# Row maxima on one core: loads of equal size from two queues in place of loads of shrinking size from one

## The chip, the cores and the metric

The kernel runs on one core of a Trainium2 chip. The metric is the device time of one execution in microseconds, taken as the median over runs. A profiled execution also has a span: the time from its first to its last recorded instruction, which is a little shorter than its device time.

## What is computed

The input has 32 x 512 x 1024 float32 values (67.11 MB). The output is the maximum over the last dimension, 32 x 512 float32 values (65.5 KB):

```
batch, seq, dim = 32, 512, 1024
x = np.random.randn(batch, seq, dim).astype(np.float32)
out = np.max(x, axis=-1).astype(np.float32)
```

There are 16,384 rows of 1024 values, and each row is read once. In what follows "a row" is a row per partition: 128 rows of the input, one on each of the 128 partitions, 4 KB each, 0.524 MB in all.

## The kernel before, in words

The 16,384 rows are dealt out so that partition p holds rows 128p to 128p+127; on each partition there are I = 128 rows to reduce, and a load of g rows reads 4g KB of contiguous memory for each partition.

The kernel is one loop over the list ROWS (line 12), which has 27 entries that begin at 10 and 13 and shrink to 1; they sum to 127. For each entry it does two things. Line 47 issues one load of g rows from SP's queue, into the next g rows of a ring of 46 rows in on-chip memory (RING, line 13; when fewer than g rows are left at the ring's end, it starts again at the ring's beginning). Line 48 reduces these g rows on VectorE (DVE) to g columns of the tile `res`. The last row is loaded in two halves of 512 values (line 58), each half is reduced by itself (line 59), and one instruction takes the larger of the two (line 60).

Two stores leave from the Activation engine's queue (ACT): line 53 stores the first 112 columns of `res` once the first 112 rows have been reduced, and line 64 stores the last 16 at the end.

Nobody writes the order of the engines by hand. A framework tracks which instruction reads and writes which part of which tile and puts in the waits. Three kinds matter here. A reduction waits for the landing of its own load. A load waits, in the queue that issues it, until the reductions that read the part of the ring it will overwrite have ended. And the framework counts landings on eight semaphores that it hands out in turn to all loads and stores, so a load also waits for the landing of the transfer eight before it. Instructions of one queue are issued in order: one that waits holds up those behind it.

Of the kernel before, what the change touches and what calls it, by code (L numbers as in the profile page):

```python
# [1 line left out]

# [4 lines left out]


F32 = mybir.dt.float32


ROWS = [10, 13, 12, 10, 9, 8, 7, 7, 6, 5, 5, 4, 4, 3, 3, 3, 3, 2, 2, 2, 2, 2, 1, 1, 1, 1, 1]
RING = 46


@with_exitstack
def kernel(
    ctx: ExitStack,
    tc: tile.TileContext,
    x: bass.AP,  # L20
    out: bass.AP,
):
    nc = tc.nc
    P = 128
    X = mybir.AxisListType.X

    xf = x.flatten_outer_dims()
    N, D = xf.shape
    H = D // 2
    I = N // P  # L30

    xr = xf.rearrange("(p i) d -> p i d", p=P)
    of = out.flatten_outer_dims()
    out_r = bass.AP(tensor=of.tensor, offset=of.offset, ap=[[I, P], [1, I]])

    once = ctx.enter_context(tc.tile_pool(name="once", bufs=1))
    ring = once.tile([P, RING, D], F32)
    res = once.tile([P, I], F32)
    part = once.tile([P, 2], F32)

    b = at = 0
    stored = 0
    for g in ROWS:
        if at + g > RING:
            at = 0
        xc = ring[:, at:at + g, :]
        nc.sync.dma_start(out=xc, in_=xr[:, b:b + g, :])
        nc.vector.reduce_max(out=res[:, b:b + g], in_=xc, axis=X)  # L48
        at += g
        b += g  # L50
        if not stored and b >= I - 16:
            stored = b
            nc.scalar.dma_start(out=out_r[:, :b], in_=res[:, :b])

    assert b == I - 1 and at + 1 <= RING
    for h in range(2):
        xh = ring[:, at, h * H:(h + 1) * H]
        nc.sync.dma_start(out=xh, in_=xr[:, b, h * H:(h + 1) * H])
        nc.vector.reduce_max(out=part[:, h:h + 1], in_=xh, axis=X)  # L59
    nc.vector.tensor_tensor(  # L60
        out=res[:, b:b + 1], in0=part[:, 0:1], in1=part[:, 1:2],
        op=mybir.AluOpType.max,
    )
    nc.scalar.dma_start(out=out_r[:, stored:], in_=res[:, stored:])


# [1 line left out]
_INS = ['x']  # L68
_OUTS = [((32, 512), 'float32')]


# [23 lines left out]
```

## Time and profile before

| what | us |
|---|---|
| median of 3 runs | 166.39 |
| lowest and highest of the runs | 165.94, 166.50 |
| device time of the profiled execution | 166.5 |
| span of the profiled execution | 164.7 |
| DVE busy within the span | 139.5 |
| DVE idle ahead of the reductions, waiting for loads | 22.7, in 6 waits |

In the profile, DVE is VectorE, SPq and ACTq are the queues from which SP and the Activation engine issue transfers, and `ring<-in_x_dram` is a load from the input into the tile `ring`. A row of the timeline has the start, the duration, the engine, the line of the code, the operation, its output and input with their shapes, and a count where several like instructions were merged into one row; brackets at its end tell how long the engine had been idle and what ended that. In the rows on DMA queues there are the number of packets, the MB and the share of the time of the 16 DMA engines that these packets took. q1 is SP's queue, q10 is ACT's. One load of g rows is 144 packets: 128, one for each partition, and 16 small ones that report completion. A row of the groups by shape has the total and the mean duration (ns) of its instructions and the idle time ahead of them.

### The profile page before, as it was taken

To read this page: it belongs to the slowest core of one execution; us is meant where nothing else is said; L and a number is where in the kernel's file an instruction comes from. 1 tells how busy PE (TensorE), PEld (TensorE's weight loads), DVE (VectorE), ACT (ScalarE), POOL (GpSimd) and SP (SyncE) were. 2 spreads that over 40 slices of the span, in tenths; PEclk is the share of its full clock that TensorE was granted. 3 is DMA by queue.
4 is the path that set the end of the run, shared out by engine and by line. 5 is a ranking of instruction groups with operands and counts; after the bars stand their busy time and mean duration, and the time that the engine had idled before them with its cause. 6 is when DMAs were issued, how large, how long until landed. Compare 5 with 4: busy or idle time off the path is not lost.

```text
span 164.7 us, 118 instructions
## 1 busy us (share of the span) xinstructions
DVE 139.5 (85%) x30; POOL 0.2 (0%) x4
## 2 busy tenths in 40 slices
DVE  0001994399989999999999989999999999999994
POOL 0000000000000000000000000000000000000000
DMA  6998999999989999999999999999999999999960
GB/s 199 438 467 376 453 465 453 436 406 394 469 388 467 444 430 430 408 438 425 439 432 425 426 431 419 428 438 409 438 430 421 427 421 421 420 418 421 408 260 2
DMA packets 4464, 67.18 MB, mean 408 GB/s; under 512 B 752, under 2 KB 752, under 8 KB 1648
## 3 DMA queue, kind: packets, MB, share of 16 engines
q1 hardware_dynamic: 4176, 67.11, 95.8%
q10 hardware_dynamic: 288, 0.07, 0.2%
HBM read 67.11 MB, written 0.07 MB: 408 GB/s over the span
## 4 chain that ended last, share of the span: by engine, by line
DMA 70%; DVE 28%; issue 0%
DMA ring<-in_x_dram 70%; DVE res L48 27%; DVE part L59 1%; DVE res L60 0%
## 5 line engine op out<-in xcount | busy, mean ns | idle before, releaser
L48 DVE TENSOR_REDUCE res<-ring 128x2 f32<-128x2048 f32 (+11 forms) x27 | 138.1, 5165 | 22.9 <-DMA ring<-in_x_dram 22.7
L59 DVE TENSOR_REDUCE part<-ring 128x1 f32<-128x512 f32 x2 | 1.3, 676 | 0.0
L60 DVE TENSOR_TENSOR res<-part 128x1 f32<-128x1 f32 x1 | 0.2, 159 | 0.0
L79 POOL MEMSET const-bfloat16-1.0<- 128x1 bf16 x1 | 0.1, 101 | 0.0
L79 POOL MEMSET const-uint8-127<- 128x1 uint8 x1 | 0.1, 101 | 0.0
L79 POOL MEMSET const-float32-0.0<- 128x1 f32 x1 | 0.1, 98 | 0.2 <-issue 0.2
L79 POOL MEMSET const-float32-1.0<- 128x1 f32 x1 | 0.1, 98 | 0.0
## 6 DMA issues: line engine op xcount, KB each, us to landing
ring<-in_x_dram SPq DMA_DIRECT2D x2, 5120.0 KB, 35.6
ring<-in_x_dram SPq DMA_DIRECT2D x2, 3584.0 KB, 33.0
ring<-in_x_dram SPq DMA_DIRECT2D x1, 6656.0 KB, 30.4
ring<-in_x_dram SPq DMA_DIRECT2D x1, 6144.0 KB, 44.4
ring<-in_x_dram SPq DMA_DIRECT2D x4, 1536.0 KB, 38.9
ring<-in_x_dram SPq DMA_DIRECT2D x2, 2560.0 KB, 38.1
ring<-in_x_dram SPq DMA_DIRECT2D x5, 1024.0 KB, 22.2
ring<-in_x_dram SPq DMA_DIRECT2D x1, 4608.0 KB, 43.1
```

What stands on the lines that cost most here:

```text
L48: nc.vector.reduce_max(out=res[:, b:b + g], in_=xc, axis=X)
L59: nc.vector.reduce_max(out=part[:, h:h + 1], in_=xh, axis=X)
L60: nc.vector.tensor_tensor(out=res[:, b:b + 1], in0=part[:, 0:1], in1=part[:, 1:2], op=mybir.AluOpType.max,)
L79: nc = _bacc.Bacc("TRN2", target_bir_lowering=False, num_devices=1)
```

## The change

The ring, the list of sizes and the two half rows are gone. There are 28 loads of four rows, through a pool of ten buffers (`bulk`), and then eight loads of two rows, through a pool of five (`tailp`). Loads alternate between the two queues: in each loop the first, third and so on are issued from SP, the second, fourth and so on from ACT. Each load has one reduction. The two stores stay on ACT's queue and store the same columns as before.

```diff
-ROWS = [10, 13, 12, 10, 9, 8, 7, 7, 6, 5, 5, 4, 4, 3, 3, 3, 3, 2, 2, 2, 2, 2, 1, 1, 1, 1, 1]
-RING = 46
...
-    b = at = 0
-    stored = 0
-    for g in ROWS:
-        if at + g > RING:
-            at = 0
-        xc = ring[:, at:at + g, :]
-        nc.sync.dma_start(out=xc, in_=xr[:, b:b + g, :])
-        nc.vector.reduce_max(out=res[:, b:b + g], in_=xc, axis=X)
-        at += g
-        b += g
-        if not stored and b >= I - 16:
-            stored = b
-            nc.scalar.dma_start(out=out_r[:, :b], in_=res[:, :b])
+    GB = 4
+    GT = 2
+    TAIL_ROWS = 16
+    NB = (I - TAIL_ROWS) // GB
+    NT = TAIL_ROWS // GT
+    SPLIT = I - TAIL_ROWS
...
+    bulk = ctx.enter_context(tc.tile_pool(name="bulk", bufs=10))
+    tailp = ctx.enter_context(tc.tile_pool(name="tailp", bufs=5))
+    respool = ctx.enter_context(tc.tile_pool(name="res", bufs=1))
...
+    for c in range(NB):
+        b = c * GB
+        xc = bulk.tile([P, GB, D], mybir.dt.float32)
+        (nc.sync, nc.scalar)[c % 2].dma_start(out=xc, in_=xr[:, b:b + GB, :])
+        nc.vector.reduce_max(
+            out=res[:, b:b + GB],
+            in_=xc,
+            axis=mybir.AxisListType.X,
+        )
...
-    assert b == I - 1 and at + 1 <= RING
-    for h in range(2):
-        xh = ring[:, at, h * H:(h + 1) * H]
-        nc.sync.dma_start(out=xh, in_=xr[:, b, h * H:(h + 1) * H])
-        nc.vector.reduce_max(out=part[:, h:h + 1], in_=xh, axis=X)
-    nc.vector.tensor_tensor(
-        out=res[:, b:b + 1], in0=part[:, 0:1], in1=part[:, 1:2],
-        op=mybir.AluOpType.max,
-    )
-    nc.scalar.dma_start(out=out_r[:, stored:], in_=res[:, stored:])
+    nc.scalar.dma_start(out=out_r[:, :SPLIT], in_=res[:, :SPLIT])
...
+    for t in range(NT):
+        b = SPLIT + t * GT
+        xt = tailp.tile([P, GT, D], mybir.dt.float32)
+        (nc.sync, nc.scalar)[t % 2].dma_start(out=xt, in_=xr[:, b:b + GT, :])
+        nc.vector.reduce_max(
+            out=res[:, b:b + GT],
+            in_=xt,
+            axis=mybir.AxisListType.X,
+        )
...
+    nc.scalar.dma_start(out=out_r[:, SPLIT:], in_=res[:, SPLIT:])
```

In the built program the queues hold, in this order: SP, 14 loads of four rows and four of two; ACT, 14 loads of four rows, two of two, the first store, two loads of two, the last store. DVE has the 28 reductions of four rows and then the eight of two, in the order of the rows. Loads and stores are counted on the eight semaphores in turn, over both queues.

More of the change, by code (lines that the diff above doesn't have):

```diff
@@ L6 @@
 from concourse._compat import with_exitstack
-F32 = mybir.dt.float32
-ROWS = [10, 13, 12, 10, 9, 8, 7, 7, 6, 5, 5, 4, 4, 3, 3, 3, 3, 2, 2, 2, 2, 2, 1, 1, 1, 1, 1]
-RING = 46
 @with_exitstack
@@ L24 @@
     P = 128
-    X = mybir.AxisListType.X
     xf = x.flatten_outer_dims()
     N, D = xf.shape
-    H = D // 2
+    assert N % P == 0
     I = N // P
@@ L34 @@
     out_r = bass.AP(tensor=of.tensor, offset=of.offset, ap=[[I, P], [1, I]])
[L36 to L39, printed above, removed]
-    b = at = 0
-    stored = 0
-    for g in ROWS:
-        if at + g > RING:
-            at = 0
-        xc = ring[:, at:at + g, :]
-        nc.sync.dma_start(out=xc, in_=xr[:, b:b + g, :])
-        nc.vector.reduce_max(out=res[:, b:b + g], in_=xc, axis=X)
-        at += g
-        b += g
-        if not stored and b >= I - 16:
-            stored = b
-            nc.scalar.dma_start(out=out_r[:, :b], in_=res[:, :b])
-    assert b == I - 1 and at + 1 <= RING
-    for h in range(2):
-        xh = ring[:, at, h * H:(h + 1) * H]
-        nc.sync.dma_start(out=xh, in_=xr[:, b, h * H:(h + 1) * H])
-        nc.vector.reduce_max(out=part[:, h:h + 1], in_=xh, axis=X)
-    nc.vector.tensor_tensor(
-        out=res[:, b:b + 1], in0=part[:, 0:1], in1=part[:, 1:2],
-        op=mybir.AluOpType.max,
-    )
-    nc.scalar.dma_start(out=out_r[:, stored:], in_=res[:, stored:])
+    GB = 4
[7 more added lines that the diff above has]
+    respool = ctx.enter_context(tc.tile_pool(name="res", bufs=1))
+    res = respool.tile([P, I], mybir.dt.float32)
+    for c in range(NB):
[18 more added lines that the diff above has]
+    nc.scalar.dma_start(out=out_r[:, SPLIT:], in_=res[:, SPLIT:])
 _INS = ['x']
```

## The prediction

> **What bounds the kernel now.** I read the page first, then the timeline, the windows by stage, the groups by shape, and the DMA queues of one short window. On the page:
>
> ```profile
> span 164.7 us, 118 instructions
> DVE 139.5 (85%) x30; POOL 0.2 (0%) x4
> DVE  0001994399989999999999989999999999999994
> DMA  6998999999989999999999999999999999999960
> q1 hardware_dynamic: 4176, 67.11, 95.8%
> ```
>
> The DMA engines are full from the second slice to the last but two: the kernel is the time to read 67.11 MB. VectorE (DVE) is nearly full, but only because it is slowed to the pace of the loads; its work is 139.5 us. q1 is SP's queue, 144 packets for each of the 29 loads. The windows by stage (window, its length, DVE busy, POOL busy, clock, DMA share, GB/s):
>
> ```profile
> 20.00:60.00 40.00, 34.58 (x4) 0.00 (x0) 1.00 1.00 432
> 60.00:100.00 40.00, 39.16 (x5) 0.00 (x0) 1.00 1.00 428
> 100.00:130.00 30.00, 29.97 (x6) 0.00 (x0) 1.00 1.00 427
> 130.00:152.00 22.00, 21.25 (x9) 0.00 (x0) 1.00 1.00 420
> ```
>
> So 420 to 432 GB/s, with the share of the engines at 1.00. What can move is the rate, and what is left to do once the data are in. For that, the timeline:
>
> ```profile
> 15.82 10.82 DVE L48 TENSOR_REDUCE res<-ring 128x10 f32<-128x10240 f32 x1 [15.82 <-DMA ring<-in_x_dram]
> 31.56 14.02 DVE L48 TENSOR_REDUCE res<-ring 128x13 f32<-128x13312 f32 x1 [4.91 <-DMA ring<-in_x_dram]
> 46.08 49.61 DVE L48 TENSOR_REDUCE res<-ring 128x12 f32<-128x12288 f32 x5 [0.50 <-DMA ring<-in_x_dram]
> 96.50 43.73 DVE L48 TENSOR_REDUCE res<-ring 128x7 f32<-128x7168 f32 x9 [0.81 <-DMA ring<-in_x_dram]
> 140.55 9.93 DVE L48 TENSOR_REDUCE res<-ring 128x3 f32<-128x3072 f32 x4 [0.33 <-DMA ring<-in_x_dram]
> 162.25 0.16 DVE L60 TENSOR_TENSOR res<-part 128x1 f32<-128x1 f32 x1
> 162.44 0.34 ACTq L64 DMA_DIRECT2D out_dram<-res  x1
> ```
>
> 1+1+5+9 = 16 reductions stand ahead of the one at 140.55, so that is load 17; loads 1 to 17 hold 112 of the 128 rows per partition. DVE waited 0.33 us for it: at 140.55 exactly 112 rows had landed and 109 had been reduced. From there DVE ends at 162.41, and the span 2.29 us later, at 164.7 (the store's issue and landing, and the program's end). The first load's landing is the other anchor: 10 rows, 5.24 MB, at 15.8.
>
> **The change, part by part.** Removed: 29 loads on SP's queue, 30 DVE instructions. Added: 28 loads of four rows (2.10 MB) and 8 of two (1.05 MB), the first, third and so on from SP, the others from ACT; one reduction for each. The groups by shape price them:
>
> ```profile
> L48 DVE TENSOR_REDUCE res<-ring 128x2 f32<-128x2048 f32 x5 | 11.2, 2280 | 0.3 <-DMA ring<-in_x_dram 0.3
> L48 DVE TENSOR_REDUCE res<-ring 128x4 f32<-128x4096 f32 x2 | 8.8, 4416 | 0.0
> ```
>
> DVE's sum: 28 x 4.416 + 8 x 2.280 = 141.9 us, 2.4 more than 139.5. By itself that is hidden: four rows take 4.42 us to reduce and 2.10 MB / 427 GB/s = 4.91 us to load, so DVE catches up with the loads until the end.
>
> The order of landing is what decides. No load of the trace shares the engines with another queue's loads, but the first store does: it is issued on ACT at 143.94, while SP's loads run. The DMA queues of the window 147.5 to 150.0 (packets, MB, share):
>
> ```profile
> q1 hardware_dynamic: 136, 0.98, 93.3%
> q10 hardware_dynamic: 134, 0.06, 8.2%
> ```
>
> 136 packets of SP's queue and 134 of ACT's, in the same 2.5 us: the engines take one packet from each in turn. The loads' packets are all alike in the new kernel (one partition's four rows, 16 KB), so a load of SP's and the next one of ACT's share the engines evenly and land together, every 2 x 4.91 = 9.8 us, SP's by about one packet the earlier: 16 KB at 427/16 = 26.7 GB/s per engine, 0.6 us. Before, loads landed one after another.
>
> The Trainium skill, "DMA: Bandwidth & Descriptors", section "Queues, rings and completion order", says that an engine drains a whole packet of some 9 to 17 descriptors from one ring before it switches. A load's share of one engine is 144/16 = 9 of the trace's packets; were that drained whole, the two would land half a period apart, which is rival B below. The row (136 against 134) looks like turns of one, and the sum goes by it.
>
> The last pair of four-row loads completes when 112 rows have landed, with nothing else ahead of it. Before, that was 140.55. Bounds from the stages' rates, over the 53.5 MB that follow the first 5.24: 15.8 + 53.5/0.432 = 139.6, and 15.8 + 53.5/0.420 = 143.2. The stage whose loads have packets nearest to 16 KB (six to three rows, 100 to 130 us) gives 427: 141.0. I take 140.55, the same bytes in the same trace, between them.
>
> From there: the reduction of load 27 can start at 140.55 - 0.6 = 139.95, the bounds being 140.55 (ACT is first, or both at once) and 135.65 (half a period of lead). Then 2 x 4.42 + 8 x 2.28 = 27.1 us back to back, to 167.0. Before, DVE ended at 162.41. So +4.6 us. The rest, the final store and the end, stays at 2.29: span 169.3.
>
> Is DVE never made to wait in these 27.1 us? The tail loads go through five buffers, so the last three wait for the reductions of the first three, which end at 139.95 + 8.83 + 2.28 = 151.1, 153.3 and 155.6, and are wanted by DVE at 160.2, 162.5 and 164.7: some 9.1 us later each. Such a load on emptying queues: the first load of the trace took 15.07 us from issue, 12.3 of them for its 5.24 MB at 427, so 2.8 + 1.05/0.427 = 5.3 us; the last one-row load of the trace, issued into a full queue, took 8.7. Both are under 9.1, so it costs nothing; were it 12 us, the end would be some 3 us later. The queue that this is moved past: on ACT the first store waits for the reduction of load 28 (148.8), and behind it wait tail loads 6 and 8. The sixth waits until 151.1 for its buffer anyway, so the store hides in that wait.
>
> The bulk loads: a load waits in its issuing queue for the landing of the load eight before it and, from the eleventh on, for the reduction of the one ten before. When a pair lands, three loads remain in each queue, 12.6 MB or 29 us of work; an issue takes 0.33 to 0.88 us on SP's queue. Hidden by these 29 us. The buffer asked for was read by a reduction which ends a period of 9.8 us less 8.8 before. The half-row loads, the part maxima and the final maximum (1.3 + 0.2 us) go; they are in the 162.41 above.
>
> The sum: the profiled execution took 166.5 us, its span 164.7, so 1.8 lie around it. 166.5 + 4.6 = 171.1; the median of the runs is 166.39, 0.1 below the profiled one, so **171.0**.
>
> **The rivals.** (A) The forecast, pairs: its own range is 169.4 to 172.6 (140.55 moved to 139.6 or 141.0, lead of 0 to 1.2 us). Against it: 136 to 134 was seen with store packets of 448 B, not with two streams of loads.
>
> (B) Staggered landing: one queue runs half a period ahead, by a late first issue on ACT or by draining whole shares. Load 27 lands at 135.65 and is done before load 28 at 140.55; then 4.42 + 18.24 to 163.2, +0.8 us: 167.2. For it: a lead of 1 us at the start, when one queue has the engines alone, becomes 2 us at the landing, since the other then gains at half rate; SP's first issue takes 0.88 us. Against it: nothing holds the two queues apart for 2.5 us at the start, and the packet counts.
>
> (C) The other side: two rings and equal packets raise the rate itself, so T0 = 140.55 comes earlier with the pairing unchanged. To win back 4.6 us over 124.75 needs 428.7 x 124.75/120.15 = 445 GB/s; from there it is not slower, and at 447, 166.5. Against it: no stage is above 432, and the engines' share is 1.00 already. At 432 it is 170.0, which is in A. The same page of the skill, section "Issuing engines are not separate DMA queues", speaks against a gain: issuing from several engines saves sequencer time only. No run here shows it for loads.
>
> (D) The two streams get in each other's way, and the rate falls to the lowest stage's 420 or under: T0 = 143.2 gives 173.7; at 415, 175.2. For it: 4 KB to 8 KB packets run at 420, so the rate is not a constant of the engines. Against it: the new packets are of the faster size.
>
> (E) The change does less than it says: the loads alternate in the program, but the engines serve ACT's ring only when SP's is empty. Then load 2 lands after SP's first four, five loads or 10.5 MB in, at 15.8 + 5.24/0.427 = 28.1, and DVE's own work from there, 27 x 4.42 + 18.24 = 137.6, ends at 165.7, still under A's 167.0. At the end SP's first two tail loads (2.10 MB, 4.9 us) pass load 28, which lands at 145.5: 4.42 + 18.24 more is 168.1, so 172.2. Against it: the packet counts.
>
> **How the numbers follow.** A 0.70, B 0.13, C 0.04, D 0.10, E 0.03. The time is A's, 171.0. The range takes in A, most of B's middle ground (a lead of up to 3 us takes 2.4 off) and the edge of D: 168.4 to 173.4. A measurement here can tell about 0.3%, 0.5 us, from no change. B at its very best is +0.5%, so slower too; no change needs B's best and a rate of 430, or C at 443 to 447; faster needs C beyond that. Faster 0.03, same 0.05, slower 0.92.
>
> **What would show it.** Right: landings of four-row loads in pairs 9.8 us apart; DVE waiting once per pair, about 1 us each; no DVE wait after the last pair; both queues with some 2,600 packets (18 loads x 144) and equal shares in each window; DVE busy without a gap for 26 to 28 us before the final store. The tail loads landing well ahead of their reductions shows the five buffers free of cost. Wrong: DVE waits once per load, not per pair (B); a rate over 440 or under 420 (C, D); a DVE wait among the last eight reductions (the tail's buffers).

## The result, and the profile after

The changed kernel takes 171.2 us (median of 4 runs, 171.16 to 171.23). The kernel before took 166.44 beside it. The ratio is 1.029, with a 95% interval of 1.0266 to 1.0314: it is slower, by 4.8 us. The profiled execution took 171.16 us, with a span of 169.4. The page of the changed kernel, in its parts on busy time, slices and DMA queues:

```profile
span 169.4 us, 142 instructions
...
DVE 140.0 (83%) x36; POOL 0.2 (0%) x4
...
DVE  0008979798997979799797979979797997999994
...
DMA  5999999999999999999999999999999999999900
...
q10 hardware_dynamic: 2880, 33.62, 47.3%
q1 hardware_dynamic: 2592, 33.56, 47.0%
```

The bytes are split evenly between the two queues, and DVE's work is what it was (140.0 against 139.5 us). The DMA row is as full as before until the last two slices, which are empty now: the last load lands at 162.1 us (160.7 before), and the span goes on after it. The windows by stage have the same rates as before, and the DMA queues of five microseconds in the middle, 60 to 65, show both queues at once:

```profile
20.00:60.00 40.00, 35.82 (x9) 0.00 (x0) 1.00 1.01 431
60.00:100.00 40.00, 35.81 (x9) 0.00 (x0) 1.00 1.00 428
100.00:130.00 30.00, 26.69 (x7) 0.00 (x0) 1.00 1.01 429
130.00:152.00 22.00, 20.06 (x6) 0.00 (x0) 1.00 1.00 420
```

```profile
q1 hardware_dynamic: 82, 1.08, 50.9%
q10 hardware_dynamic: 81, 1.07, 50.0%
```

So nothing was lost in the rate (432, 428, 427, 420 before). What changed is when the data are handed to DVE. From the timeline:

```profile
13.38 8.74 DVE L47 TENSOR_REDUCE res<-xc 128x4 f32<-128x4096 f32 x2 [13.38 <-DMA xc<-in_x_dram]
23.17 8.74 DVE L47 TENSOR_REDUCE res<-xc 128x4 f32<-128x4096 f32 x2 [1.04 <-DMA xc<-in_x_dram]
...
130.89 8.74 DVE L47 TENSOR_REDUCE res<-xc 128x4 f32<-128x4096 f32 x2 [1.04 <-DMA xc<-in_x_dram]
140.69 8.74 DVE L47 TENSOR_REDUCE res<-xc 128x4 f32<-128x4096 f32 x2 [1.06 <-DMA xc<-in_x_dram]
149.35 17.63 DVE L59 TENSOR_REDUCE res<-xt 128x2 f32<-128x2048 f32 x8
...
167.01 0.35 ACTq L65 DMA_DIRECT2D out_dram<-res  x1
```

DVE starts every 9.8 us, does two reductions, and waits 1.05 us. That two loads land together is also seen in the queues: once the first eight loads are out, the next is issued as soon as the load eight before it lands, so these two issues show the landings of loads 19 and 20, 0.18 us apart:

```profile
101.55 0.33 SPq L46 DMA_DIRECT2D xc<-in_x_dram  x1
...
101.73 0.33 ACTq L46 DMA_DIRECT2D xc<-in_x_dram  x1
```

The last start of a pair is at 140.69, when 112 rows have landed, as at 140.55 before. From there eight rows of the last pair and the 16 of the tail are reduced back to back, to 166.98. Before, DVE had three rows in hand at that moment, and the 16 to come, and ended at 162.41. The difference of these two ends is 4.6 of the 4.8 us.

One rule serves for all the runs below. DVE ends at the latest of these sums, one for each load: the time at which it lands, and the reductions from it to the last. Here the sum that decides is that of the 27th load: 140.69 + 8.74 + 17.63 = 167.06 (166.98 in the trace, where successive instructions overlap by some hundredths).

### The profile page after: what moved, and what is told of

The parts are those of the page before. It is cut to its first block, busy times and chain, and to the rows that moved or that the text cites. A ratio compares the mean times of both kernels' runs of the same rounds, so it can differ in the third digit from the quotient of the medians.

```text
span 169.4 us, 142 instructions
## 1 busy us (share of the span) xinstructions
DVE 140.0 (83%) x36; POOL 0.2 (0%) x4
## 4 chain that ended last, share of the span: by engine, by line
DMA 82%; DVE 14%; DVEq 1%; SPq 0%; issue 0%
DMA xc<-in_x_dram 82%; DVE res L59 9%; DVE res L47 5%; DVEq L91 1%; SPq L46 0%
## 5 line engine op out<-in xcount | busy, mean ns | idle before, releaser
L47 DVE TENSOR_REDUCE res<-xc 128x4 f32<-128x4096 f32 x28 | 122.4, 4414 | 27.0 <-DMA xc<-in_x_dram 27.0
L59 DVE TENSOR_REDUCE res<-xt 128x2 f32<-128x2048 f32 x8 | 17.6, 2276 | 0.0
```

The source lines that it names most:

```text
L47: nc.vector.reduce_max(out=res[:, b:b + GB], in_=xc, axis=mybir.AxisListType.X,)
L59: nc.vector.reduce_max(out=res[:, b:b + GT], in_=xt, axis=mybir.AxisListType.X,)
```

## The experiments

The runs came in three groups, each with runs of the kernel before beside it; its median was 165.89 in the first group, 166.88 in the second and 166.51 in the third. So the ratios compare across groups better than the times.

### One queue, the same loads

```diff
-        (nc.sync, nc.scalar)[c % 2].dma_start(out=xc, in_=xr[:, b:b + GB, :])
+        nc.sync.dma_start(out=xc, in_=xr[:, b:b + GB, :])
...
-        (nc.sync, nc.scalar)[t % 2].dma_start(out=xt, in_=xr[:, b:b + GT, :])
+        nc.sync.dma_start(out=xt, in_=xr[:, b:b + GT, :])
```

> All 36 loads from SP's queue, sizes and buffers as in the changed kernel. If the pairing of landings is the cost: four-row loads land one by one every 4.9 us, DVE waits some 0.5 us for each; load 28 lands at about 140.7, its reduction ends at 145.0, eight more of 2.2 us end at 162.7, and with the 2.4 us from there to the end the span is 165.1, the time 166.9. If it is the sizes that cost (equal loads, whichever queue): 171.2 as with two queues.

Measured: 166.83 us, ratio 1.0056 (1.0041 to 1.0071). Its timeline at the end:

```profile
135.31 4.42 DVE L47 TENSOR_REDUCE res<-xc 128x4 f32<-128x4096 f32 x1 [0.47 <-DMA xc<-in_x_dram]
140.21 4.42 DVE L47 TENSOR_REDUCE res<-xc 128x4 f32<-128x4096 f32 x1 [0.48 <-DMA xc<-in_x_dram]
144.55 15.47 DVE L59 TENSOR_REDUCE res<-xt 128x2 f32<-128x2048 f32 x7
...
160.20 2.29 DVE L59 TENSOR_REDUCE res<-xt 128x2 f32<-128x2048 f32 x1 [0.18 <-DMA xt<-in_x_dram]
```

Load 27 is done when load 28 lands at 140.2, so one reduction of four rows (4.4 us) is off the end. DVE even waits 0.18 us for the last load: the kernel is bound by the loads to the end, plus one reduction of two rows. It ends at 162.49, 4.5 us ahead of the changed kernel.

### The kernel before, from two queues

```diff
-    for g in ROWS:
+    for n, g in enumerate(ROWS):
...
-        nc.sync.dma_start(out=xc, in_=xr[:, b:b + g, :])
+        (nc.sync, nc.scalar)[n % 2].dma_start(out=xc, in_=xr[:, b:b + g, :])
...
-        nc.sync.dma_start(out=xh, in_=xr[:, b, h * H:(h + 1) * H])
+        (nc.scalar, nc.sync)[h].dma_start(out=xh, in_=xr[:, b, h * H:(h + 1) * H])
```

> The ring and the sizes of the kernel before, the loads issued from SP and ACT in turn. If the engines take one packet of each queue in turn, whatever its size: the loads of 10 and 13 rows land together at 31.5 us, the next two at 58.3; DVE is never idle from 58.3 and ends 139.5 - 24.8 = 114.7 us later, at 173; span 175.3, time 177.1. If the queues share the bytes evenly: the first reduction starts at 28.0, and the time is some 175.8. If two queues cost nothing with these sizes: 166.4.

Measured: 176.41 us, ratio 1.0639 (1.0623 to 1.0655). The timeline:

```profile
31.56 24.75 DVE L48 TENSOR_REDUCE res<-ring 128x10 f32<-128x10240 f32 x2 [31.56 <-DMA ring<-in_x_dram]
58.78 112.52 DVE L48 TENSOR_REDUCE res<-ring 128x12 f32<-128x12288 f32 x25 [2.48 <-DMA ring<-in_x_dram]
171.23 1.27 DVE L59 TENSOR_REDUCE part<-ring 128x1 f32<-128x512 f32 x2
```

The first reduction starts at 31.56, where the load of 13 rows landed before, though its own load has only 10; by shares of bytes it would have started at 28.0, by the estimate above. So the engines give both queues one packet in turn, and packets of 40 KB and of 52 KB count alike. DVE starts 15.7 us later than before and is then the bound: from 58.78 it never waits. The loads themselves end some 12 us before it, at 160.7.

### A half load's lead, by a small load at the head of ACT's queue

```diff
+    head = respool.tile([P // 2, 128], mybir.dt.float32)
+    nc.scalar.dma_start(out=head, in_=xf[:P // 2, :128])
+
     for c in range(NB):
```

> The changed kernel with one small extra load (64 partitions of 512 B, never read) at the head of ACT's queue: 4 packets on each engine, half of a load's 8, and hardly any bytes. If the engines take packets in turn: SP's queue is ahead by 4 packets from then on, loads land one by one every 4.9 us, DVE waits once for each, and the time is 166.9 as with one queue. If the queues share by bytes or by time: the pairs stay, 171.2. If a cost of two queues other than the pairing exists, it is left over 166.9.

Measured: 170.76 us, ratio 1.0293 (1.0276 to 1.031), no gain. But the lead was not a half. The timeline:

```profile
8.64 4.42 DVE L50 TENSOR_REDUCE res<-xc 128x4 f32<-128x4096 f32 x1 [8.64 <-DMA xc<-in_x_dram]
18.78 8.75 DVE L50 TENSOR_REDUCE res<-xc 128x4 f32<-128x4096 f32 x2 [5.72 <-DMA xc<-in_x_dram]
...
136.31 13.07 DVE L50 TENSOR_REDUCE res<-xc 128x4 f32<-128x4096 f32 x3 [1.06 <-DMA xc<-in_x_dram]
149.31 17.63 DVE L62 TENSOR_REDUCE res<-xt 128x2 f32<-128x2048 f32 x8
```

The first load lands alone, and then pairs follow, of load 2 with load 3 and so on: SP was ahead by a whole load. The DMA queues of 1 to 5 us show 67 packets of SP's, some four on each engine, and none of ACT's, where the changed kernel has 37 and 31; the small load's four data packets and its completion packet on each engine, taken in turn with SP's, make up the rest of a load's eight or so. Why ACT's queue came in late here was not tried. The new pairs end at the same time by the rule: 136.31 + 13.07 + 17.63 = 167.0. As a test of the half lead it failed; it was made again, below.

### One pool for all loads

```diff
-    bulk = ctx.enter_context(tc.tile_pool(name="bulk", bufs=10))
-    tailp = ctx.enter_context(tc.tile_pool(name="tailp", bufs=5))
+    bulk = ctx.enter_context(tc.tile_pool(name="bulk", bufs=12))
...
-        xt = tailp.tile([P, GT, D], mybir.dt.float32)
+        xc = bulk.tile([P, GB, D], mybir.dt.float32)
+        xt = xc[:, :GT, :]
```

> The changed kernel with one pool of 12 buffers for all loads, so that no tail load waits for the reduction of another tail load, and the first store goes behind all loads on ACT's queue. If the wait of the last three loads for their buffers costs nothing, as predicted: 171.2, with DVE's last ten reductions back to back as before and the last load landing at about 160.4. If that wait or the store in ACT's queue is part of the 4.8 us: up to 1.5 us less.

Measured: 171.29 us, ratio 1.0325 (1.031 to 1.034). Its window from 140 to 160 us, and that of the changed kernel:

```profile
140.00:160.00 20.00, 19.18 (x7) 0.00 (x0) 1.00 1.00 415
...
140.00:160.00 20.00, 19.31 (x7) 0.00 (x0) 1.00 0.99 388
```

The loads run at 415 GB/s there, against 388, and after 160 next to nothing is left of them. It is no faster for that: DVE has its last ten reductions back to back in both. The five tail buffers do hold the loads back, and it is hidden.

### A lead in the middle, by a small store on ACT's queue

```diff
             axis=mybir.AxisListType.X,
         )
+        if c == 0:
+            nc.scalar.dma_start(out=out_r[:P // 2, :GB], in_=res[:P // 2, :GB])
```

> The changed kernel with one small store (64 partitions of 16 B, values that the later store writes again) on ACT's queue behind its second load: 4 packets on each engine, half of a load's 8. If the engines take packets in turn: the first four loads land in pairs, and from some 25 us on SP's loads are half a load ahead, so that DVE waits once per load, 0.5 us each; load 27 is done before load 28 lands, and the time is 166.9, as with one queue. If the turns go by bytes or time: pairs to the end, 171.2.

Measured: 169.36 us, ratio 1.0151 (1.0115 to 1.0186), halfway between one queue and the changed kernel. A load that waits for the landing of the load eight before it is issued at once when that lands, so the issues of the two queues show the landings. The timeline of the two queues, in four short windows, and of DVE at the end:

```profile
85.47 0.33 ACTq L46 DMA_DIRECT2D xc<-in_x_dram  x1
...
89.12 0.33 SPq L46 DMA_DIRECT2D xc<-in_x_dram  x1
...
95.25 0.33 ACTq L46 DMA_DIRECT2D xc<-in_x_dram  x1
...
98.91 0.33 SPq L46 DMA_DIRECT2D xc<-in_x_dram  x1
...
134.35 13.07 DVE L47 TENSOR_REDUCE res<-xc 128x4 f32<-128x4096 f32 x3 [1.05 <-DMA xc<-in_x_dram]
147.34 17.63 DVE L61 TENSOR_REDUCE res<-xt 128x2 f32<-128x2048 f32 x8
```

SP's load lands 3.65 us after ACT's and 6.13 before the next of ACT's; of a period of 9.78 that is five eighths, a lead of five packets where four were meant (the store has a completion packet too). So the turns go by packets, as expected. The time is not that of one queue, for a reason that the expectation had left out: the queue that leads is already at its next load, and this takes engine time from the load that DVE needs first. Load 26 lands at 134.3 here and at 130.4 from one queue, and 134.35 + 13.07 + 17.63 = 165.05 decides. A lead of exactly half a load was not run.

### The list of the kernel before, each size split over two queues

```diff
-ROWS = [10, 13, 12, 10, 9, 8, 7, 7, 6, 5, 5, 4, 4, 3, 3, 3, 3, 2, 2, 2, 2, 2, 1, 1, 1, 1, 1]
+ROWS = [5, 5, 7, 6, 6, 6, 5, 5, 5, 4, 4, 4, 4, 3, 4, 3, 3, 3, 3, 2, 3, 2, 2, 2, 2, 2, 2, 1, 2, 1, 2, 1, 2, 1,
+        1, 1, 1, 1, 1, 1, 1, 1, 1, 1, 1, 1, 1, 1, 1]
...
-        nc.sync.dma_start(out=xc, in_=xr[:, b:b + g, :])
+        (nc.sync, nc.scalar)[n % 2].dma_start(out=xc, in_=xr[:, b:b + g, :])
```

> Two queues in turn, ring and two half rows as in the kernel before, but each size of its list split into two loads, one for each queue (5 and 5 for 10, 7 and 6 for 13, and so on). If two queues cost only what the size of a pair costs: the pairs land as the single loads did before, the time is that of the kernel before or up to 1 us more (52 instructions on DVE in place of 30). If two queues cost something of their own: clearly over 167.

Measured: 172.42 us, ratio 1.0337 (1.0291 to 1.0383): the first branch of the expectation failed. Up to about 97 us DVE's waits end within 0.6 us of those of the kernel before (15.93, 31.92, 46.36 and 97.02, against 15.82, 31.56, 46.08 and 96.50). Then come the DMA queues of the window 130 to 133, and rows of the timeline:

```profile
q10 hardware_dynamic: 338, 1.24, 103.6%
q1 hardware_dynamic: 1, 0.00, 0.0%
```

```profile
126.91 0.82 ACTq L48 DMA_DIRECT2D ring<-in_x_dram  x2
...
130.69 1.28 SPq L48 DMA_DIRECT2D ring<-in_x_dram  x3
...
138.52 3.41 DVE L49 TENSOR_REDUCE res<-ring 128x2 f32<-128x2048 f32 x2 [4.03 <-DMA ring<-in_x_dram]
```

SP's queue moved nothing for 3 us while ACT's, with loads that DVE needs later, had the engines to itself. Each load waits for the landing of the transfer eight before it, counted over both queues; SP's next three loads were all issued from 130.7 on, after such a landing (of a load of ACT's, at 130.6), behind ACT's. DVE then waits 4.03 us for one of them.

### Pairs of equal loads

```diff
-ROWS = [10, 13, 12, 10, 9, 8, 7, 7, 6, 5, 5, 4, 4, 3, 3, 3, 3, 2, 2, 2, 2, 2, 1, 1, 1, 1, 1]
+ROWS = [5, 6, 6, 5, 5, 4, 4, 3, 3, 3, 2, 2, 2, 2, 2, 2, 1, 1, 1, 1, 1, 1, 1, 1]
...
+        for queue in (nc.sync, nc.scalar):
+            xc = ring[:, at:at + g, :]
+            queue.dma_start(out=xc, in_=xr[:, b:b + g, :])
```

> Two queues, pairs of equal loads (5 and 5, 6 and 6, 6, 5, 5, 4, 4, 3, 3, 3, 2 six times, 1 eight times), no half rows; a ring as in the kernel before. If the loss of the kernel with pairs of halves came from its unequal pairs, which let one queue run empty while the other ran ahead: here both queues hold the same number of loads and packets, the pairs land together to the end, and the time is that of the kernel before plus 0 to 1 us (a last pair of two rows in place of a last half row). If two queues cost something of their own, or the limit of eight transfers in flight over both queues does: over 2% more again, with waits of DVE of several us in the last 40.

Measured: 169.18 us, ratio 1.0145 (1.0118 to 1.0172). Rows of its timeline:

```profile
15.88 10.88 DVE L47 TENSOR_REDUCE res<-ring 128x5 f32<-128x5120 f32 x2 [15.88 <-DMA ring<-in_x_dram]
...
70.44 41.33 DVE L47 TENSOR_REDUCE res<-ring 128x5 f32<-128x5120 f32 x10 [1.53 <-DMA ring<-in_x_dram]
...
141.97 20.27 DVE L47 TENSOR_REDUCE res<-ring 128x2 f32<-128x2048 f32 x16 [0.49 <-DMA ring<-in_x_dram]
162.39 2.35 DVE L47 TENSOR_REDUCE res<-ring 128x1 f32<-128x1024 f32 x2 [0.15 <-DMA ring<-in_x_dram]
```

DVE's last waits are 0.50, 0.49 and 0.15 us now, so that the long wait did come from the unequal pairs. But it takes 2.7 us more than the kernel before, over the 0 to 1 expected. In the profiles its loads fall behind bit by bit: the pairs that complete 10, 54 and 112 rows land at 15.9, 70.4 and 142.0, and the kernel before has these rows at 15.8, 69.8 (a load issued at 26.67 that took 43.10 us to land) and 140.5. From 60 us on its windows by stage are at 421, 423 and 413 GB/s, against 428, 427 and 420; its loads, and so its packets, are about half as large. That makes 1.4 us. Another 0.9 lie behind: from the landing of 112 rows to its end DVE takes 22.8 us here and 21.9 before, and two reductions follow its last wait. No run has this list on one queue, so it is not shown how much of the 2.7 us the second queue itself costs.

### Only the end shrinks, and the one-queue kernels again

The first of these kernels is the kernel before with a list of 25 fours, 4 threes, 5 twos and 5 ones; it was run in two groups. The other two are the one-queue kernel and the changed kernel, again, all in the third group.

```diff
-ROWS = [10, 13, 12, 10, 9, 8, 7, 7, 6, 5, 5, 4, 4, 3, 3, 3, 3, 2, 2, 2, 2, 2, 1, 1, 1, 1, 1]
+ROWS = [4] * 25 + [3] * 4 + [2] * 5 + [1] * 5
```

> One queue, ring and half rows as in the kernel before, but with 25 loads of four rows at the head in place of its loads of 10 down to 4; then 4 of three, 5 of two, 5 of one. If only the loads at the end count: the same time as the kernel before, within 0.5 us, and DVE waits from the first load on, 0.5 us each. If the large loads at the start are worth something (by the rate of their large packets, 432 against 428): 0.5 to 1.2 us more.

> One queue, 25 loads of four rows and the shrinking end of the kernel before. If the 1.1 us that it lost before came from one late stretch (the third load landed 1.3 us late in that profile, all loads after it shifted by the same), and not from the sizes: the same as the kernel before within 0.5 us where that stretch is missing, and under the kernel above. If the small loads at the start cost by themselves: 1.1 us more again.

> The changed sizes from SP's queue alone, beside the next two on one chip. If the last load of two rows and DVE's backlog ahead of it are all that it loses to the kernel before: 0.9 us more than that one, as measured already.

> The changed kernel itself, beside the one-queue kernel on the same chip. If pairing is what the second queue costs: 4.3 us over the one-queue kernel (the reduction that waits for the last four-row landing is followed by one more of 4.4 us), 171.2 where the kernel before takes 166.4.

| kernel | us | ratio to the kernel before | interval |
|---|---|---|---|
| only the end shrinks | 167.96 | 1.0065 | 1.004 to 1.009 |
| only the end shrinks, again | 167.89 | 1.0081 | 1.0055 to 1.0106 |
| one queue, again | 167.74 | 1.0083 | 1.0051 to 1.0115 |
| the changed kernel, again | 171.80 | 1.0315 | 1.029 to 1.0341 |

The second queue costs 171.80 - 167.74 = 4.06 us on one chip; 4.3 was expected. By the times, the shrinking end brings nothing over the one-queue kernel there. Where the two lose 1.2 to 1.4 us to the kernel before, their profiles tell in part. With the shrinking end 112 rows have landed at 141.4 (140.55 in the kernel before), and DVE needs 21.9 us from there, as before; from one queue with equal loads they have landed at 141.1, and DVE needs 22.3. So most is lost ahead of the 112 rows, and in these profiles the shrinking end is worth some 0.4 us. The start of the first kernel's first run:

```profile
12.99 4.42 DVE L48 TENSOR_REDUCE res<-ring 128x4 f32<-128x4096 f32 x1 [0.44 <-DMA ring<-in_x_dram]
19.18 4.42 DVE L48 TENSOR_REDUCE res<-ring 128x4 f32<-128x4096 f32 x1 [1.76 <-DMA ring<-in_x_dram]
24.08 4.42 DVE L48 TENSOR_REDUCE res<-ring 128x4 f32<-128x4096 f32 x1 [0.48 <-DMA ring<-in_x_dram]
```

One early load lands 1.3 us late and shifts all that follow. The two other profiles have a smaller one (waits of 1.31 and 1.21 us, at 13.85 and 28.56, in place of some 0.47); the first run of the one-queue kernel has not, and it too took 0.9 us more than the kernel before. The late stretch was there in both runs of this kernel, so its expected absence didn't come. Nor is the kernel before free of one: its load of nine rows lands 11.6 us after the load of ten (at 69.8 and 58.2 by its trace), which had taken 12.1, so it is some 0.7 us late. How much of the loss is such stretches, and how much the rate of the large early packets (432 against some 428 GB/s), is not settled.

### Two rows throughout

```diff
-    GB = 4
+    GB = 2
...
-    bulk = ctx.enter_context(tc.tile_pool(name="bulk", bufs=10))
+    bulk = ctx.enter_context(tc.tile_pool(name="bulk", bufs=20))
```

> The changed kernel with 56 loads of two rows in place of its 28 of four, through 20 buffers. If the size of the pair sets the cost: a pair is now four rows; the last one lands at about 160.2, two reductions later DVE ends at 164.6, time 168.8 at the rate of 428 GB/s; less by 2.4 us than the changed kernel. If packets of 8 KB run at 420 GB/s, as in the stage of 130 to 152 us of the kernel before: 3 us more, 171.8.

Measured: 170.99 us, ratio 1.025 (1.0215 to 1.0284). The windows by stage, and two rows of the timeline:

```profile
20.00:60.00 40.00, 35.22 (x17) 0.00 (x0) 1.00 1.01 418
60.00:100.00 40.00, 36.09 (x17) 0.00 (x0) 1.00 1.01 420
100.00:130.00 30.00, 26.82 (x13) 0.00 (x0) 1.00 1.01 421
```

```profile
143.41 4.48 DVE L47 TENSOR_REDUCE res<-xc 128x2 f32<-128x2048 f32 x2 [0.48 <-DMA xc<-in_x_dram]
...
160.32 6.67 DVE L59 TENSOR_REDUCE res<-xt 128x2 f32<-128x2048 f32 x3 [0.27 <-DMA xt<-in_x_dram]
```

Packets of 8 KB run at 420 and 421 GB/s from 60 to 130 us, where those of 16 KB run at 428 and 429; the 418 ahead of that has a late stretch in it (a wait of 1.38 us at 23.95, and a second of 0.75 at 123.58, in place of 0.49). So 112 rows land at 143.4 in place of 140.7, 1.1 us of it by these two stretches, and what the smaller pair takes from DVE's backlog (4.5 us left of it in place of 8.7) is given back by the loads: DVE waits until 160.3, has three more reductions to do, and ends where the changed kernel does. Of the two branches of the expectation the second, with the low rate, is nearer (171.8; the first had 168.8), but the late stretches have a part in that.

## Why the prediction was right

- The step that decides, what is unreduced when 112 rows have landed, was right: pairs every 9.8 us with one wait of about 1 us each, DVE busy from the last pair to the end, the rate unchanged. One queue with the same loads takes most of it away: in the third group, 4.06 of the 5.29 us between the changed kernel (171.80) and the kernel before (166.51).
- Two terms were off, and it is luck that they cancelled. The lead of SP's load over ACT's was put at 0.6 us, one packet; the landings, seen in the issues that they release, are 0.18 us apart. With that, and with the 112 rows complete some 0.3 us later than taken, the last pair began at 140.69, not 139.95. And 27.1 us of reductions are 26.3: they overlap, so that one of four rows lasts 4.41 us but the next starts 4.33 after it, and one of two rows lasts 2.28 with the next at 2.19. The span was put at 169.3 and is 169.4 by these errors, +0.7 and -0.8, and 0.1 more behind the last reduction.
- Three of its readings and sums are wrong, without effect on the forecast. By the terms that it names, A's own range ends at 172.1 (171.0 + 0.45 + 0.6), not 172.6; at 447 GB/s C gives 165.9, not 166.5; and SP's first issue takes 0.37 us, the one of 0.88 is its fourth.
- The tail's buffers: the last load was issued at 156.04 and took 6.1 us of the 8.7 that DVE left it; 5.3 to 8.7 had been estimated. Hidden, as said; without that wait the kernel is no faster.
- Rival B, the staggered landing, was mis-sized. It said 167.2 for a lead of half a period, and the run with a lead of five eighths gave a ratio of 1.0151, or some 168.9 for a kernel before of 166.4. The two leads are not the same, but the run shows what B had left out: the leading queue goes on to its next load while the other's is still under way. From one queue a load has the engines to itself, and so the loads land one by one, 4.89 us apart.
- In these traces the turns are of one packet: the two loads of a pair land 0.18 us apart, not half a period; loads of 10 and of 13 rows land together; and a store of five small packets on each engine put its queue five packets behind. The rule of the Trainium skill ("DMA: Bandwidth & Descriptors", section "Queues, rings and completion order") that an engine drains a whole packet of some 9 to 17 descriptors of one ring before it switches is not what they show, if a packet of the trace is one descriptor, as the prediction took it; the measurement decides.
- Rivals C and D fell with the windows (431, 428, 429, 420), and E with the pairs.

What is shown: the second queue's cost with these loads, the turns by packet, the harmlessness of the tail's buffers. Not settled: how the remaining 0.9 to 1.4 us between one queue of equal loads and the kernel before divide between late stretches, the rate and the end. None of the versions beat the kernel before.

## What to carry to other kernels

The loads filled the DMA engines already, and a second issuing queue brought no rate here and spoiled the order: two loads that share the engines both land when the later one would have, so the consumer gets the data in lumps of two. Such a cost is read at the end: for each load add its landing and the work left from it on, and take the latest sum. If two queues are wanted for another reason, keep the loads small and equal at the end, and see that neither queue can run empty; that was 169.18 us here, against 171.8 for the changed kernel on the same chip.

## What was not expected

- The engines' turns count packets, not bytes: loads of 40 KB and 52 KB packets landed at the same time (31.56 us). A store of 64 x 16 B moved one queue against the other for the rest of the kernel, by 6.13 us.
- A limit on transfers in flight that is counted over both queues can empty one of them: 338 packets of the one and a single one of the other in 3 us, and a wait of 4.03 us.
- The rate differs with the size of the loads: 420 and 421 GB/s with packets of 8 KB, 428 and 429 with 16 KB, in the same stretch of 60 to 130 us. Loads of two rows also have twice as many completion packets for the same bytes; which of the two it is was not tried.
